# Down projection of a fused attention and FFN block: three groups of 3, 4 and 4 row blocks instead of 2, 3, 3, 3, and other places for its first weight operands

## Chip, cores and metric

One NeuronCore of one Trainium2 chip runs the whole program in one launch. The metric is device time in microseconds (us), median of several runs. Before the change it is 1469.17 us, three runs, 1468.47 to 1473.25.

## What is computed

One block of a diffusion model on 1024 tokens of width 1024, with 256 context tokens: modulation vectors from a condition, neighbourhood attention over a 16 x 64 grid with 16 heads, and a gated FFN of width 2816 with a depthwise convolution. Only the FFN's second product is touched by the change:

```python
def conv_ffn(h, w_up, conv_w, conv_b, w_down):
    a, g = jnp.split(h @ w_up, 2, axis=-1)
    return (a * jax.nn.gelu(dwconv_centred(g, conv_w, conv_b), approximate=False)) @ w_down

x = x + g1 * y
x = x + g2 * conv_ffn(modulate(rms_norm(x, norm2), sh2, sc2), *ffn)
```

All is in float32. Each operand of a large product is split into a rounded high part and a low rest, and a product is three matmuls: high by high, high by low, low by high.

## The kernel before, in words

Both FFN products are done in the seven-product scheme for 2 x 2 blocks (Strassen and Winograd): seven block products with pre-added operands instead of eight. Seven products of one kind are called **ops** here, by the numbers 1 to 7 in the program.

**Up projection** (`up_part`, `up_mm`, line 744). It runs over 11 pairs of hidden row blocks (`i`) and two halves (`part` 1 is g, 0 is a); each op is 12 matmuls into a PSUM bank. Its moving operands `b<op>h`, `b<op>l` stay in SBUF all through: ops 1, 2 and 5 and so on fill 12 places of tag `bA`, then 10 places of `bB`, then 6 of `wa`. A place comes free when the last pair (`i` = 10) has used it. In the last pair PE runs ops 1, 2, 5, 7, 6, then 3, 4. `conv` (line 791) is six taps on DVE for each hidden block, lines 766 and 770 combine the products, and `finish` (804 to 813) writes the seven pre-added forms of the result to `act_dram`.

**Down projection** (`down_mm`, lines 912 to 914). It contracts over 11 row blocks `c`, in groups of `GROUPS` = 2, 3, 3, 3. For each group the ops run in the order `DORD` = 2, 1, 5, 6, 3, 7, 4; an op has four output tiles `j`, and for each the blocks of the group, three matmuls each, into one bank. So an op of a group of n blocks is 12n matmuls, the whole 924. At the end of each bank the sum is moved into `acc` in SBUF: by ACT in the first group for ops 2, 5, 6, 4 (919), else by a DVE add (931). Two sets of four banks take turns; the fourth of both sets lies in one tile, `dx`, which also holds the up projection's `sw`. In the last group DVE and POOL multiply by the gate (927, 928) and POOL issues the output's DMAs (929).

Operands come from two helpers. `prep_a` (872 to 874) loads `da` from `act_dram` (256 KB each, SP queue), ACT rounds it (873), DVE or POOL subtracts to get the low part (874); places `bA`, three ops ahead. `prep_b` (898, 899) takes the raw weights `dr` (loaded at 865, 512 KB each, into places `x1` and `wa`), pre-adds in place on DVE (890, 892, 894, 896), rounds on ACT and subtracts; `db` lies in places `bB`, two ops ahead. DVE makes the low parts for ops 2, 1 and 7, POOL for 5, 6, 3 and 4. While POOL does that, in the last op of the last group but one it also multiplies by the gate and adds the residual (933, 934, eight instructions).

What sets the order on each engine: the program is recorded as written and a scheduler then orders each engine's instructions by its own estimate; each engine runs its queue in order. A place of a tag is given out in turn, and who takes it next waits until its last reader is done.

## Time and profile before

| | |
|---|---|
| runs, median | 1469.17 us (1468.47, 1473.25, 1469.17) |
| the profiled execution | 1474.2 us |
| its span, first to last instruction | 1472.4 us |
| granted TensorE clock, mean | 0.977 |
| DVE busy | 1194.9 us (81%) |
| ACT busy | 746.1 us (51%) |
| POOL busy | 795.0 us (54%) |

The profile is one execution on the chip. Times are from the span's start. A row of the timeline gives start, duration, engine, line, operation, `out<-in`, and in brackets the idle time ahead of it with what ended it. Matmuls overlap, so their start-to-start distance counts, not the printed duration. The down projection is what runs after 1231.83 us.

### The profile page before, as it was taken

What the parts mean: (1) busy time and instruction counts of PE and PEld (TensorE: products, weight loads), DVE (VectorE), ACT (ScalarE), POOL (GpSimd) and SP (SyncE); (2) the same over time, 40 slices, a digit from 0 to 9 for tenths busy, and PEclk for the clock granted to TensorE, in tenths of its full rate; (3) what the DMA queues carried; (4) which work ended last, traced back from release to release, by engine and by line L of the source; (5) the groups of instructions that cost most, each with busy time, mean ns of one, the idle gap of its engine ahead of it and who ended that gap; (6) DMA issues with size and microseconds to landing.
All of it is one profiled execution on the core that took longest, in us unless ns stands there. A gap on an engine that the chain in (4) does not pass through costs nothing. (4 is left out here: it accounts for less than half of the span.)

```text
span 1472.4 us, 22076 instructions
## 1 busy us (share of the span) xinstructions
PE 1371.8 (93%) x7396; PEld 1196.7 (81%) x7396; DVE 1194.9 (81%) x2375; ACT 746.1 (51%) x1617; POOL 795.0 (54%) x687
## 2 busy tenths in 40 slices
PE   6699999999999999998996999999999998999996
PEld 2589889898989899897885777888878876788885
DVE  6788878888888878876579889888888778778877
ACT  6665645555555656654466534444334335545430
POOL 1554644544454546744358645555455545277596
PEclk9899999999999999999998999999999999999998
DMA  9611221313131202253142233333332234644336
GB/s 316 175 37 51 73 81 52 97 48 104 46 104 51 76 14 73 71 129 97 30 128 87 95 100 108 108 108 108 108 108 99 102 116 152 233 145 127 122 98 103
DMA packets 84825, 150.12 MB, mean 102 GB/s; under 512 B 9944, under 2 KB 49000, under 8 KB 84712
## 3 DMA queue, kind: packets, MB, share of 16 engines
q1 hardware_dynamic: 82984, 145.57, 31.1%
q0 software_dynamic: 1728, 3.15, 1.6%
q8 instruction: 58, 0.95, 0.3%
q14 instruction: 55, 0.45, 0.1%
HBM read 115.91 MB, written 32.78 MB: 101 GB/s over the span
## 5 line engine op out<-in xcount | busy, mean ns | idle before, releaser
L692 POOL TENSOR_TENSOR u<-ur,u 128x512 fp32r<-128x512 f32 x154 | 229.4, 1504 | 189.5 <-ACT u L691 181.1
L419 POOL TENSOR_TENSOR p<-p,m 128x640 f32<-128x640 f32 (+1 forms) x128 | 157.3, 1230 | 157.8 <-DVE m L415 121.0
L303 PE MATMUL pq<-wh,hth 128*128 128x384 f32 (+1 forms) x640 | 219.8, 343 | 14.7 <-DVE kn L342 12.9
L307 PE MATMUL pq<-wh,htl 128*128 128x384 f32 (+1 forms) x640 | 215.3, 336 | 2.0 <-DVE htl L196 1.0
L305 PE MATMUL pq<-wl,hth 128*128 128x384 f32 (+1 forms) x640 | 214.9, 336 | 0.5 <-POOL wl L149 0.5
L414 ACT ACTIVATE p<-p,m 128x640 f32<-128x640 f32 (+1 forms) x128 | 102.9, 804 | 83.8 <-DVE m L412 74.4
L691 ACT ACTIVATE u<-ur 128x512 fp32r<-128x512 f32 x154 | 93.1, 627 | 97.4 <-PE sw L744 38.8
L303 PEld LDWEIGHTS pq<-wh,hth 128*128 128x128 f32 x640 | 125.1, 195 | 20.6 <-DVE kn L342 9.3
L327 POOL TENSOR_TENSOR qss<-qss,mhalf 128x4 f32<-128x4 f32 (+1 forms) x80 | 79.9, 999 | 96.9 <-DVE qss L326 82.7
L307 PEld LDWEIGHTS pq<-wh,htl 128*128 128x128 f32 x640 | 124.6, 195 | 2.5 <-DVE htl L196 2.5
L305 PEld LDWEIGHTS pq<-wl,hth 128*128 128x128 f32 x640 | 124.9, 195 | 1.6 <-issue 0.9
L791 DVE SCALAR_TENSOR_TENSOR y<-g,cw,y 128x896 f32<-128x896 f32 (+1 forms) x132 | 104.7, 858 | 21.2 <-ACT y L785 21.2
L899 POOL TENSOR_TENSOR db<-dr,db 128x512 fp32r<-128x512 f32 x44 | 65.6, 1512 | 54.6 <-ACT db L898 44.9
L451 PE MATMUL po<-pt,v 128*128 128x256 f32 x352 | 93.1, 292 | 2.2 <-DVE pt L439 2.2
L450 PE MATMUL po<-pt,v 128*128 128x256 f32 x352 | 93.9, 290 | 0.1
L412 DVE CUSTOM_DVE_ANT_0 p<-s,bias 128x640 f32<-128x640 f32 x96 | 78.4, 816 | 9.4 <-PE s L401 8.8
L898 ACT ACTIVATE db<-dr 128x512 fp32r<-128x512 f32 x77 | 47.3, 629 | 74.7 <-PE dx L914 37.3
L874 POOL TENSOR_TENSOR da<-da 128x512 fp32r<-128x512 f32 x44 | 67.9, 1591 | 29.1 <-ACT da L873 29.0
L438 ACT ACTIVATE pt<-pl 128x384 fp32r<-128x384 f32 (+1 forms) x128 | 58.0, 461 | 46.3 <-PE pl L431 45.3
L473 DVE SCALAR_TENSOR_TENSOR macc<-mr,cs,macc 128x256 f32<-128x256 f32 x112 | 65.4, 584 | 12.3 <-DMA mr<-in_w_mod_dram 11.5
L439 DVE TENSOR_TENSOR pt<-pl,pt 128x384 fp32r<-128x384 f32 (+1 forms) x128 | 65.4, 516 | 6.6 <-ACT pt L438 6.2
L451 PEld LDWEIGHTS po<-pt,v 128*128 128x128 f32 x352 | 66.6, 189 | 3.9 <-DVE pt L439 3.5
(272 smaller groups left out, 4163.8 us busy)
## 6 DMA issues: line engine op xcount, KB each, us to landing
ur<-in_w_up_dram SPq DMA_DIRECT2D x44, 512.0 KB
da<-act_dram SPq DMA_DIRECT2D x77, 256.0 KB
mr<-in_w_mod_dram SPq DMA_DIRECT2D x128, 128.0 KB
dr<-in_w_down_dram SPq DMA_DIRECT2D x22, 512.0 KB
wraw<-in_w_qkv_dram SPq DMA_DIRECT2D x56, 192.0 KB
mraw<-in_w_mod_dram SPq DMA_DIRECT2D x16, 512.0 KB
act_dram<-sa SPq DMA_DIRECT2D x11, 512.0 KB
act_dram<-y SPq DMA_DIRECT2D x11, 512.0 KB
```

The costliest lines, as they stand in the source:

```text
L303: PE.matmul(pq[:, c0:], hth[t][:, k, :], wh[:, c0:], start=(k == 0), stop=False)
L305: PE.matmul(pq[:, c0:], hth[t][:, k, :], wl[:, c0:], start=False, stop=False)
L307: PE.matmul(pq[:, c0:], htl[t][:, k, :], wh[:, c0:], start=False, stop=(k == KC - 1))
L327: POOL.tensor_tensor(ss[:, 4 - n:], ss[:, 4 - n:], mhalf[:, 4 - n:], ALU.pow)
L412: DVE.tensor_tensor_reduce(out=dst, in0=src, in1=bb, scale=1.0, scalar=3e38, op0=ALU.add, op1=ALU.min, accum_out=m[:, 0:1])
L414: ACT.activation(w[:, :n], w[:, :n], AF.Exp, bias=m[:, 0:1], scale=-1.0, accum_out=m[:, 1:2])
L419: POOL.tensor_tensor(w[:, :n], w[:, :n], m[:, 2:3].broadcast_to([P, n]), ALU.mult)
L450: PE.matmul(po, v, th[:, j].rearrange("p a b -> p (a b)"), start=(m == 0), stop=False)
L451: PE.matmul(po, v, tl[:, j].rearrange("p a b -> p (a b)"), start=False, stop=(m == len(blks) - 1))
L691: ACT.activation(s[:, 0], r[op], AF.Copy)
L692: POOL.tensor_tensor(s[:, 1], r[op], f(s[:, 0]), ALU.subtract)
L791: DVE.scalar_tensor_tensor(o, i, w, o, ALU.mult, ALU.add)
```

## The change

The 11 row blocks go in groups of 3, 4 and 4. The `db` operands of the very first op lie in `bA` (the places of the up projection's ops 1 and 2) and no longer in `bB`. Only three blocks of the next group are loaded at op 6; a fourth follows after op 4's operands.

```diff
-GROUPS = [2, 3, 3, 3]
+GROUPS = [3, 4, 4]
...
         if op == RL and n + 1 < len(groups):
-            for c in groups[n + 1]:
+            for c in groups[n + 1][:3]:
                 load_raw(c)
         for c in groups[n]:
-            s = usb.tile([P, 2, HALF], F32R, tag="bB", bufs=10, name=f"db{c}_{op}")
+
+            tag, bufs = ("bA", 12) if q == 0 else ("bB", 10)
+            s = usb.tile([P, 2, HALF], F32R, tag=tag, bufs=bufs, name=f"db{c}_{op}")
...
             opb[op, c] = s
+        if op == DORD[-1] and n + 1 < len(groups):
+            for c in groups[n + 1][3:]:
+                load_raw(c)
```

The lines behind it move by two to five: 890 becomes 892, 899 becomes 901, 912 to 914 become 917 to 919, 931 becomes 936. The matmuls stay 924, the loads 22 and 77; the moves into `acc` go from 112 to 84, all 28 of them DVE adds.

How the order changes, in three places. **DVE where the down projection begins.** `y_1` are the taps of the last pair's convolution, `db_2` and `da_2` the low parts of op 2's operands. Before:

```order
L874 TENSOR_TENSOR da_1_13569<-da_1_13569 128x512
L791 SCALAR_TENSOR_TENSOR y_1_13289<-g_1_13287,cw,y_1_13289 128x128x7
L791 SCALAR_TENSOR_TENSOR y_1_13289<-g_1_13287,cw,y_1_13289 128x112
L791 SCALAR_TENSOR_TENSOR y_1_13289<-g_1_13287,cw,y_1_13289 128x15
L766 TENSOR_TENSOR tmp_0_13427<-pa_2_13426,tmp_0_13427 128x512
L874 TENSOR_TENSOR da_1_13573<-da_1_13573 128x512
L791 SCALAR_TENSOR_TENSOR y_1_13289<-g_1_13287,cw,y_1_13289 128x112
L791 SCALAR_TENSOR_TENSOR y_1_13289<-g_1_13287,cw,y_1_13289 128x15
L791 SCALAR_TENSOR_TENSOR y_1_13289<-g_1_13287,cw,y_1_13289 128x128x7
L770 TENSOR_TENSOR y_0_13288<-tmp_0_13427,y_0_13288 128x512
L899 TENSOR_TENSOR db_2_13549<-dr_1_13543,db_2_13549 128x512
L899 TENSOR_TENSOR db_2_13552<-dr_1_13547,db_2_13552 128x512
```

Now, a little earlier in the queue (`y_0` are the taps of the block before):

```order
L901 TENSOR_TENSOR db_2_13553<-dr_1_13543,db_2_13553 128x512
L901 TENSOR_TENSOR db_2_13556<-dr_1_13547,db_2_13556 128x512
L892 TENSOR_TENSOR dr_0_13680<-dr_0_13680 128x512
L791 SCALAR_TENSOR_TENSOR y_0_13288<-g_0_13286,cw,y_0_13288 128x112
L791 SCALAR_TENSOR_TENSOR y_0_13288<-g_0_13286,cw,y_0_13288 128x15
L901 TENSOR_TENSOR db_2_13559<-dr_1_13551,db_2_13559 128x512
L791 SCALAR_TENSOR_TENSOR y_0_13288<-g_0_13286,cw,y_0_13288 128x128x7
L764 TENSOR_TENSOR g_1_13287<-sw,tmp_1_13293 128x512
L874 TENSOR_TENSOR da_2_13571<-da_2_13571 128x512
L874 TENSOR_TENSOR da_2_13575<-da_2_13575 128x512
```

The three `db_2` stand ahead of all six taps of `y_1` and of line 770; `db_1` now is what follows line 770 and the last `da_1`.

**SP's queue, the first group's `da`.** Before, the loads for six ops stand together, ahead of the last `y_0` store:

```order
L872 DMA da_1_13573<-act_dram 128x512
L872 DMA da_5_13577<-act_dram 128x512
L872 DMA da_5_13581<-act_dram 128x512
L872 DMA da_6_13602<-act_dram 128x512
L872 DMA da_6_13606<-act_dram 128x512
L872 DMA da_3_13658<-act_dram 128x512
L872 DMA da_3_13662<-act_dram 128x512
L872 DMA da_7_13700<-act_dram 128x512
L872 DMA da_7_13704<-act_dram 128x512
L804 DMA act_dram<-y_0_13288 128x512
```

Now only ops 2, 1 and 5 stand there, since nine `da` and three `db` fill the 12 places:

```order
L872 DMA da_5_13603<-act_dram 128x512
L804 DMA act_dram<-y_0_13288 128x512
...
L865 DMA dr_0_14173<-in_w_down_dram 128x1024
L812 DMA act_dram<-sa_13526 128x1024
L805 DMA act_dram<-y_1_13289 128x1024
L872 DMA da_6_13628<-act_dram 128x512
L872 DMA da_6_13632<-act_dram 128x512
L872 DMA da_6_13636<-act_dram 128x512
```

Op 6's `da` moved behind seven weight loads (six left out) and two stores of the up projection's last pair.

**POOL in the last group, where op 3 ends.** Before:

```order
L929 DMA out_dram<-acc_13585 16x8x512
L928 TENSOR_TENSOR acc_13586<-acc_13586,g2b 128x512
L899 TENSOR_TENSOR db_3_14983<-dr_1_14447,db_3_14983 128x512
L929 DMA out_dram<-acc_13587 16x8x512
L899 TENSOR_TENSOR db_3_14986<-dr_1_14451,db_3_14986 128x512
L928 TENSOR_TENSOR acc_13588<-acc_13588,g2b 128x512
L874 TENSOR_TENSOR da_4_15053<-da_4_15053 128x512
L929 DMA out_dram<-acc_13586 16x8x512
```

Now:

```order
L901 TENSOR_TENSOR db_3_14876<-dr_1_14179,db_3_14876 128x512
L874 TENSOR_TENSOR da_3_14801<-da_3_14801 128x512
L874 TENSOR_TENSOR da_3_14805<-da_3_14805 128x512
L874 TENSOR_TENSOR da_3_14809<-da_3_14809 128x512
L934 DMA out_dram<-acc_13608 16x8x512
L901 TENSOR_TENSOR db_3_14879<-dr_1_14183,db_3_14879 128x512
L901 TENSOR_TENSOR db_3_14882<-dr_1_14451,db_3_14882 128x512
L934 DMA out_dram<-acc_13610 16x8x512
L901 TENSOR_TENSOR db_4_15037<-dr_1_14175,db_4_15037 128x512
```

Two of the gate multiplications and two output DMAs of op 1 stand further ahead, among op 6's operands, and four splits of each kind stand where three stood.

## The prediction

> **What bounds the kernel now.** I read the busy shares first, then the down projection in stretches (columns: PE, PEld, DVE, ACT, POOL busy with counts, granted clock, DMA share, GB/s), then PE's own waits after 1170 us.

> ```profile
> PE 1371.8 (93%) x7396; PEld 1196.7 (81%) x7396; DVE 1194.9 (81%) x2375; ACT 746.1 (51%) x1617; POOL 795.0 (54%) x687
> ```
> ```profile
> 1231.80:1238.10 6.30, 0.41 (x2) 0.00 (x0) 6.30 (x5) 5.14 (x10) 6.20 (x5) 0.84 0.11 42
> 1238.10:1242.60 4.50, 4.44 (x9) 2.82 (x10) 4.50 (x5) 0.45 (x1) 2.79 (x2) 0.50 0.00 0
> ...
> 1260.00:1434.00 174.00, 174.00 (x769) 144.10 (x768) 134.04 (x167) 83.47 (x136) 116.29 (x81) 1.00 0.42 134
> ...
> 1445.50:1451.40 5.90, 5.89 (x14) 4.64 (x15) 5.83 (x5) 0.19 (x1) 5.48 (x5) 0.52 0.20 20
> ```
> ```profile
> PE dpo L913 <- DVE db L899: 5.9, 1, 5.9
> PE dx L912 <- DVE acc L931: 5.5, 1, 5.5
> PE dx L912 <- DVE tmp L766: 1.7, 1, 1.7
> ...
> PE dpq L913 <- POOL db L899: 0.5, 1, 0.5
> ```

> PE is the bound: from 1260 to 1434 it never stops, 769 matmuls in 174 us, **0.2263 us** each. Neither weights nor DMA limit that stretch. What can be won lies in the two ends, so I add up PE's lost time there from its timeline.

> ```profile
> 1231.83 0.39 PE L912 MATMUL dpo<-db,da 128*128 128x512 f32 x1
> 1238.12 0.79 PE L913 MATMUL dpo<-db,da 128*128 128x512 f32 x1 [5.91 <-DVE db L899]
> ...
> 1245.98 0.39 PE L744 MATMUL pa<-b3h,u 128*128 128x512 f32 x1
> ...
> 1253.91 0.39 PE L914 MATMUL dpq<-db,da 128*128 128x512 f32 x1
> 1256.00 0.50 PE L912 MATMUL dx<-db,da 128*128 128x512 f32 x1 [1.70 <-DVE tmp L766]
> ...
> 1439.63 0.39 PE L914 MATMUL dpo<-db,da 128*128 128x512 f32 x1
> 1445.51 0.79 PE L912 MATMUL dx<-db,da 128*128 128x512 f32 x1 [5.49 <-DVE acc L931]
> ...
> 1451.43 0.39 PE L914 MATMUL dtr<-db,da 128*128 128x512 f32 x1
> ...
> 1466.39 0.39 PE L914 MATMUL dx<-db,da 128*128 128x512 f32 x1
> ```

> From 1231.83 to 1466.39 are 234.6 us. 924 down matmuls and 24 of up ops 3 and 4 are 947 steps of 0.2263, 214.3 us; **20.3 us are lost**. At the beginning: the wait, 6.29 - 0.23 = 6.06; then 24 matmuls (5.43) take 7.86 at the halved clock of the second stretch, 2.43 lost; together 8.5. At `dx`: 2.09 - 0.23 = 1.86. At the end: 0.6 on POOL's split, 5.88 - 0.23 = 5.65 at `dx`, then 14 steps (3.17) take 5.92, 2.75 lost; together 9.0. The last 0.9 is spread.

> **The change, part by part.**

> *First weight operands.* The wait at 1231.83 is for `db_2`'s low part, and DVE's own queue made it late:

> ```profile
> 1220.40 0.69 DVE L890 TENSOR_TENSOR dr<-dr 128x512 f32<-128x512 f32 x1 [0.97 <-DMA dr<-in_w_down_dram]
> 1221.01 1.66 DVE L791 SCALAR_TENSOR_TENSOR y<-g,cw,y 128x112 f32<-128x112 f32 x3
> ...
> 1225.42 0.69 DVE L874 TENSOR_TENSOR da<-da 128x512 fp32r<-128x512 f32 x1 [0.95 <-ACT da L873]
> 1226.55 1.68 DVE L791 SCALAR_TENSOR_TENSOR y<-g,cw,y 128x896 f32<-128x896 f32 x3 [0.44 <-ACT y L785]
> ...
> 1229.90 4.82 DVE L791 SCALAR_TENSOR_TENSOR y<-g,cw,y 128x112 f32<-128x112 f32 x3
> 1234.64 1.75 DVE L770 TENSOR_TENSOR y<-tmp,y 128x512 f32<-128x512 f32 x1
> 1236.32 3.44 DVE L899 TENSOR_TENSOR db<-dr,db 128x512 fp32r<-128x512 f32 x2
> ```
> ```profile
> 1228.12 9.40 POOL L874 TENSOR_TENSOR da<-da 128x512 fp32r<-128x512 f32 x6 [10.14 <-ACT da L873]
> ```

> Three taps take 1.66 us with POOL quiet and 4.82 beside POOL's splits (1.57 each); the adds of two SBUF tiles go from 0.69 to 1.75. After the change the three `db_2` (0.6 apart, 1.8) go into DVE's gaps of 0.97, 0.95 and 0.44, so `y_1`'s taps start at about 1226.6 as now. Behind them stand taps 1.68, line 766 0.6, three taps 1.66, `da_2` and three `da_1` 2.4, line 770 0.6: 6.94, to 1233.5. POOL cannot slow them before about 1233, for its first work, op 5's `da`, is now rounded on ACT behind two `db_1`, the second in the place that up op 6 holds to 1232. `db_1`'s first low part comes at 1234.2 alone, and up to 2.8 later if that split, line 770 and the last `da_1` meet POOL (1.1 more for most of them). PE needs it after nine `dpo` and three `dtr` matmuls, 1231.83 + 12 x 0.2263 = 1234.5. So the new wait is 0 to 2.5 us; I take 1.5, and no halved clock, since the 1.70 us wait at 1256.00 was followed by none. **Saved: 8.5 - 1.5 = 7.0.**

> *`dx` behind the up projection.* Now DVE has op 7's first pre-add ahead of the read of `sw` (line 766), and that pre-add waits for POOL's tenth split: 1233.2 + 10 x 1.57 = 1248.9, then 1.7 and 0.7: 1251.3. PE comes after 79 matmuls, 1231.83 + 17.9 + 1.5 = 1251.2. Between 0 and 4 us (POOL at 1.9 a split, as in a row below); I take 1.0. **Saved: 0.9.**

> *Op 6's `da` behind SP's stores.* Its DMA can go at about 1255, after the `y_1` store that waits for DVE's last line 770.

> ```profile
> 1269.02 1.01 SPq L872 DMA_DIRECT2D da<-act_dram  x2
> ```
> ```profile
> 1272.36 1.28 ACT L873 ACTIVATE da<-da 128x512 fp32r<-128x512 f32 x2 [0.60 <-DMA da<-act_dram]
> ```

> The second of these was issued by 1270.0 and used at 1272.36: at least 2.4, at most 3.4 us. With two stores and three loads in the way I put it at 1259.5 and POOL's split at 1261.4. PE has 45 matmuls after `dx` (op 2's rest, op 5, op 1's last bank), 10.2 us from 1251.8: 1262. Cost 0 with 0.6 us to spare; upper bound 4.

> *Group size.* 28 DVE adds go, 0.68 each (19 us of DVE):

> ```profile
> L931 DVE TENSOR_TENSOR acc<-dtr,acc x33: 674/678/692, 1258.3 to 1443.4; 128x512 f32<-128x512 f32 x33
> ```

> They lie beside a PE that never stops, so by themselves they are worth nothing. Four blocks leave less room: 12 places are three ops of `da`, 10 are two and a half of `db`. In the middle groups a `db` place comes back about 13 us before its next use (one op of 48 matmuls, 10.9, plus the last bank), and POOL makes eight splits for ops 5, 6 and 3 in that time, 8 x 1.44 (116.29 / 81) = 11.5: hidden, at most 2 us per group at 1.75 a split. The fourth block's weights are asked for after op 4's operands, an op or more ahead.

> *The end.* What held PE at 1445.51:

> ```profile
> 1423.12 1.76 DVE L894 TENSOR_TENSOR dr<-dr 128x512 f32<-128x512 f32 x1 [1.19 <-POOL db L899]
> ...
> 1433.02 8.46 DVE L894 TENSOR_TENSOR dr<-dr 128x512 f32<-128x512 f32 x1 [2.93 <-POOL db L899]
> ...
> 1444.77 0.68 DVE L931 TENSOR_TENSOR acc<-dx,acc 128x512 f32<-128x512 f32 x1
> ```
> ```profile
> 1399.40:1434.48 35.08, 35.08 (x156) 28.89 (x154) 26.67 (x27) 12.62 (x21) 35.08 (x26) 1.00 0.36 99
> ```
> ```profile
> 1433.22 1.88 POOL L899 TENSOR_TENSOR db<-dr,db 128x512 fp32r<-128x512 f32 x1
> ...
> 1440.00 1.70 POOL L929 DMA_DIRECT2D out_dram<-acc  x1
> ```

> One pre-add stood 8.46 us, exactly while POOL had no gap, and the move out of `dx` stood behind it. POOL was behind because the last group's 24 splits share it with the residual, gate and output work. That extra work stays the same, but the group's PE time grows from 84 x 3 to 84 x 4 matmuls (57 to 76 us). POOL's string is 35.08 / 26 = 1.35 us each; from the residual of the third bank (2 us ahead of the group) to op 3's last `db` are 33 instructions, 44.6 us, 42.6 into the group; PE wants it at 4 x 10.9 + 2.0 = 45.5. So op 3 does not wait, and op 7 has 10.9 us behind it. Between two uses of `dx` lie three banks, 27 matmuls (6.1 us) before and 36 (8.15) now. The same 8.46 us pre-add would hold PE 5.49 - 2.04 = 3.45 us. Bounds 0 and 9; I take 3.4. **Saved: 5.6.**

> [...]

> **Sum:** 7.0 + 0.9 + 5.6 = 13.5 off the profiled execution's 1474.2 us: 1460.7. That execution stands 5.0 above the median. If its excess is one of the waits removed here, runs after come out at 1460.7; if it lies ahead of 1231, at 1455.7. I say **1460**, nearer the first, as the waits are what I can see.

> **Rivals.**
> - *The wait moves to the next operands of the first group:* `db_1` (2.5 instead of 1.5), `dx` (4 instead of 1) and op 6's `da` (2 instead of 0): 6 more, 1466. For it: POOL at 1.9 a split. Against: POOL starts later than now.
> - *The end stays as it is:* 9.0 instead of 3.4, 1466.
> - *Slower: DVE starves behind POOL at both ends.* Mechanism: the 8.46 us row. At the beginning POOL has six splits in a row (1233.2 to 1242.6); a `db_1` held for all of it gives 8.1 us and 2.75 of clock, 9.3 more than taken. At the end the string is four instructions longer, 9.0 + 5.4 instead of 3.4, 11 more. 1481. It decides once a pre-add stands longer than `dx`'s 8.15 us. Against: in 174 us without a stop DVE got in after one POOL instruction nearly always.
> - *The early splits are not early,* because their weights land late: 8.5 stays, 1468.

> **Chances.** Forecast (1454 to 1464.5) 0.58, first rival 0.16, second 0.14, slower 0.08, last 0.04. The range 1454 to 1469 leaves out the slower case and the tails. About 0.3% (4.4 us) is what a measurement can tell from no change. Faster by more, below 1464.8: the forecast and a good third of the rivals at 1466, 0.70; within 0.19; slower 0.11.

> **What would show it.** Right: PE's first `dpo` has no wait, its first wait is for `db_1`, under 3.4 us, with clock 1.00; POOL's first split starts near 1233; PE runs through groups 2 and 3; a `dx` wait near the end under 4 us. Wrong: a wait of PE on `da` or POOL inside the 4-block groups, a stretch at 0.50 near 1238, or a DVE pre-add over 8 us with PE idle behind it.

## The result, and the profile after

The changed kernel takes 1463.95 us (median of 13 runs, 1458.21 to 1468.27); the kernel before, beside it, 1472.22 us (13 runs, 1467.62 to 1474.77). The ratio is 0.9948, 95% interval 0.9935 to 0.9961: 7.7 us faster by the ratio. The profiled execution took 1463.59 us, its span is 1461.8. Of the experiments' executions one, of e2, took 7620 us; the ratios leave it out. Busy shares hardly moved; DVE's busy time fell from 1194.9 to 1184.4 us, by less than the 19 us of the 28 adds:

```profile
PE 1368.4 (94%) x7396; PEld 1193.9 (82%) x7396; DVE 1184.4 (81%) x2347; ACT 741.8 (51%) x1617; POOL 797.4 (55%) x687
```

PE's waits in the down projection, all of them (line, what it waited for, us in total, times, longest):

```profile
PE dx L917 <- DVE acc L936: 2.7, 1, 2.7
PE dpq L917 <- DVE tmp L766: 2.0, 1, 2.0
PE dx L917 <- DVE tmp L766: 1.3, 1, 1.3
PE sw L744 <- DVE tmp L778: 0.2, 1, 0.2
```

The wait of 5.9 us at the first `dpo` is gone, and none for `db_1` has come. The one near the end is 2.7 instead of 5.5 us. New is a wait for a bank, `dpq`. PE's timeline at these places, and four stretches (columns as in the prediction; the third from the end is the granted clock):

```profile
1230.17 0.39 PE L917 MATMUL dpo<-db,da 128*128 128x512 f32 x1
...
1248.80 0.53 PE L917 MATMUL dpq<-db,da 128*128 128x512 f32 x1 [2.03 <-DVE tmp L766]
...
1253.97 0.50 PE L917 MATMUL dx<-db,da 128*128 128x512 f32 x1 [1.26 <-DVE tmp L766]
...
1418.90 0.50 PE L917 MATMUL dx<-db,da 128*128 128x512 f32 x1 [2.73 <-DVE acc L936]
...
1455.80 0.39 PE L919 MATMUL dx<-db,da 128*128 128x512 f32 x1
```
```profile
1230.17:1248.00 17.83, 16.36 (x70) 12.61 (x68) 14.12 (x16) 6.63 (x12) 15.87 (x9) 1.00 0.38 128
1248.80:1252.50 3.70, 3.70 (x9) 2.59 (x9) 3.70 (x4) 0.35 (x1) 2.16 (x2) 0.54 0.57 231
1254.00:1415.00 161.00, 161.00 (x710) 133.28 (x711) 123.33 (x130) 75.89 (x129) 113.28 (x79) 1.00 0.47 151
1418.90:1423.34 4.44, 4.44 (x12) 3.49 (x13) 4.44 (x6) 2.18 (x4) 2.28 (x3) 0.62 0.79 139
```

From 1230.17 to 1455.80 are 225.6 us. The same 214.3 us of matmuls as in the prediction leave **11.3 us lost**, against 20.3 before: 9.0 less. The other 1.66 us of the two executions' difference lie ahead: the first down matmul started at 1230.17, not at 1231.83. The lost time after: at the beginning the `dpq` wait (2.19), nine matmuls at the half clock behind it (1.50), `dx` (1.63), 0.38 at up op 4 and 1.0 spread, 6.7 in all; at the end `dx` (2.89) and twelve matmuls that took 4.44 us instead of 2.72, 4.6 in all. In the middle PE never stops for 161 us. What stands behind the wait near the end, DVE's pre-add and its move out of `dx`, and two output DMA issues of POOL ahead of them:

```profile
1409.68 7.97 DVE L896 TENSOR_TENSOR dr<-dr 128x512 f32<-128x512 f32 x1 [4.57 <-POOL db L901]
...
1418.17 0.68 DVE L936 TENSOR_TENSOR acc<-dx,acc 128x512 f32<-128x512 f32 x1
```
```profile
1402.70 1.01 POOL L934 DMA_DIRECT2D out_dram<-acc  x1
...
1405.95 1.14 POOL L934 DMA_DIRECT2D out_dram<-acc  x1
```

### The profile page after: what moved, and what is told of

It reads as the page before. It is cut to its first block, busy times and chain, and to the rows that moved or that the text cites. A ratio compares the mean times of both kernels' runs of the same rounds, so it can differ in the third digit from the quotient of the medians.

```text
span 1461.8 us, 22048 instructions
## 1 busy us (share of the span) xinstructions
PE 1368.4 (94%) x7396; PEld 1193.9 (82%) x7396; DVE 1184.4 (81%) x2347; ACT 741.8 (51%) x1617; POOL 797.4 (55%) x687
## 5 line engine op out<-in xcount | busy, mean ns | idle before, releaser
L791 DVE SCALAR_TENSOR_TENSOR y<-g,cw,y 128x896 f32<-128x896 f32 (+1 forms) x132 | 101.7, 835 | 21.2 <-ACT y L785 21.2
L874 POOL TENSOR_TENSOR da<-da 128x512 fp32r<-128x512 f32 x44 | 71.0, 1658 | 36.3 <-ACT da L873 36.3
```

Of the source, the lines that this page charges most:

```text
L791: DVE.scalar_tensor_tensor(o, i, w, o, ALU.mult, ALU.add)
```

## The experiments

Twelve kernels were run. How they stand, with three numbers of each profiled execution: its first down matmul, PE's lost time as above, and the tail from the start of the last matmul to the end of the span.

| kernel | ratio to before (95%) | first | lost | tail |
|---|---|---|---|---|
| before | 1 | 1231.83 | 20.3 | 6.0 |
| whole change | 0.9948 (0.9935 to 0.9961) | 1230.17 | 11.3 | 6.0 |
| e1, groups alone | 0.9996 (0.9983 to 1.0010) | 1234.74 | 19.2 | 6.1 |
| e2, places alone | 0.9998 (0.9985 to 1.0010) | 1230.66 | 18.7 | 6.0 |
| e5, e2 without POOL's early work | 0.9938 (0.9922 to 0.9954) | 1229.97 | 11.7 | 6.0 |
| e3, `dx` as two tiles | 0.9962 (0.9949 to 0.9975) | 1230.08 | 10.1 | 8.7 |
| e7, op 3's `db` on DVE | 0.9966 (0.9951 to 0.9982) | 1232.54 | 16.9 | 6.0 |
| e6, e3 and e7 together | 0.9926 (0.9908 to 0.9944) | 1234.21 | 7.2 | 7.2 |
| e9, without op 1's output DMAs | 0.9938 (0.9918 to 0.9957) | 1231.27 | 10.6 | 6.1 |
| e4, without six pre-adds | 0.9940 (0.9928 to 0.9953) | 1234.12 | 7.5 | 6.1 |
| e8, e6 and three pre-adds on POOL | 0.9930 (0.9910 to 0.9950) | 1232.77 | 9.2 | 7.2 |

The first down matmul comes anywhere from 1229.97 to 1234.74, though these kernels are nearly alike up to there. One execution's span therefore says little about 4 us; lost time and tail of one trace, and the ratio over several runs, say more. The sum of lost time and tail, taken from that of before, foretells the ratio within 2 us (0.0014) for every kernel but e4.

**The two parts of the change.** e1 leaves the first `db` in its old place, e2 leaves the groups:

```diff
e1: -            tag, bufs = ("bA", 12) if q == 0 else ("bB", 10)
    +            tag, bufs = "bB", 10
e2: -GROUPS = [3, 4, 4]
    +GROUPS = [2, 3, 3, 3]
```

> Only the groups of 3, 4 and 4; the first db operands lie in bB as in the kernel before. In the two traces PE's lost time from the first dpo to the last matmul is 20.3 us before and 11.3 after (beginning 10.9 and 6.7, end 9.0 and 4.6). Theory (two separate gains: places at the beginning, longer groups at the end): PE stands at its first dpo again, 5 to 8 us behind DVE's db low part, with the clock at half afterwards, and the end loses about 4.6 as with the whole change; time 3 to 5 us under the kernel before, ratio about 0.997. Rival (the groups bring it all, by fewer moves into acc and less work on DVE): ratio 0.995 as with the whole change.

> Only the places of the first db operands; groups of 2, 3, 3 and 3 as before. Theory: no wait at the first dpo and no stretch at half clock right behind it; the end as before, a dx wait of about 5.5 us with 2.75 of half clock; 3 to 6 us under the kernel before, ratio about 0.997, and the savings of this and of the groups alone add up to the 8.3 us of the whole change within 2. Rival (the wait moves to db_1 or dx when a group is only two blocks, 6 dpo and 24 dtr matmuls): no gain, ratio 1.000.

Neither is shown to be faster than before. In e1 the wait at `dpo` is longer than before (8.4 us, not 5.9), since three `db_2` now stand behind the taps, and so is the one at `dx` (6.2, not 5.5). In e2 the wait is gone at `dpo` and back at `db_1`: the rival. PE's two longest waits in e1, then in e2:

```profile
PE dpo L918 <- DVE db L901: 8.4, 1, 8.4
PE dx L917 <- DVE acc L936: 6.2, 1, 6.2
```
```profile
PE dtr L918 <- DVE db L901: 5.6, 1, 5.6
PE dx L917 <- DVE acc L936: 5.5, 1, 5.5
```

So the gain is not a sum of two. What the two parts do together shows on DVE and POOL where POOL's first split meets DVE's row. In e2 (DVE, then POOL):

```profile
1227.47 0.67 DVE L766 TENSOR_TENSOR tmp<-pa,tmp 128x512 f32<-128x512 f32 x1
1228.08 1.73 DVE L874 TENSOR_TENSOR da<-da 128x512 fp32r<-128x512 f32 x1
1229.73 2.69 DVE L791 SCALAR_TENSOR_TENSOR y<-g,cw,y 128x112 f32<-128x112 f32 x2
...
1236.68 3.42 DVE L901 TENSOR_TENSOR db<-dr,db 128x512 fp32r<-128x512 f32 x2
```
```profile
1227.96 8.25 POOL L874 TENSOR_TENSOR da<-da 128x512 fp32r<-128x512 f32 x5 [11.15 <-ACT da L873]
```

And after the whole change (the first line is an edge of the convolution):

```profile
1228.55 0.27 DVE L791 SCALAR_TENSOR_TENSOR y<-g,cw,y 128x15 f32<-128x15 f32 x1
1228.71 0.71 DVE L874 TENSOR_TENSOR da<-da 128x512 fp32r<-128x512 f32 x1
...
1230.98 0.70 DVE L770 TENSOR_TENSOR y<-tmp,y 128x512 f32<-128x512 f32 x1
1231.58 0.71 DVE L874 TENSOR_TENSOR da<-da 128x512 fp32r<-128x512 f32 x1
1232.18 1.91 DVE L901 TENSOR_TENSOR db<-dr,db 128x512 fp32r<-128x512 f32 x3
```
```profile
1229.61 5.63 POOL L874 TENSOR_TENSOR da<-da 128x512 fp32r<-128x512 f32 x1 [13.29 <-ACT da L873]
```

In e2 the two took turns: DVE's subtractions in these rows lasted 1.73 and 1.7 us, POOL's 1.65. After the change DVE ran on at 0.70 and POOL's *first* subtraction stood for 5.63 us, until DVE paused at 1234.09. The three `db_1` took 1.91 us and PE waited for none. Whether POOL's work is what holds `db_1` in e2 was tried by leaving it out, in e2's kernel:

```diff
+            if n or op in DA:
                 (DVE if op in DA else POOL).tensor_tensor(s[:, 1], f(s[:, 1]), f(s[:, 0]), ALU.subtract)
```

> The places alone (groups of 2, 3, 3 and 3) as in the second experiment, and in the first group the low parts of da for ops 5, 6, 3 and 4 are left out (POOL's eight subtractions; those parts of the sums are not computed rightly). With the places alone PE waited 5.6 us for db_1, whose DVE queue ran beside POOL's first subtractions from 1227.96 on. Theory (POOL's start ahead of DVE's row is what made db_1 late; where the first group has three blocks POOL starts inside DVE's row and is the one that waits): without those subtractions DVE's queue runs at 0.6 us each, the db_1 wait is under 1.5 us, no half clock there; 6 to 9 us under the kernel before, ratio 0.994 to 0.996. Rival (DVE's queue is too long for two blocks in any case, or ACT is late): a db_1 wait of 4 us or more, ratio 1.000.

As the theory had it: no wait for `db_1` at all; the ratio is 0.9938 (0.994 to 0.996 expected). With two blocks DVE's queue was short enough where POOL stayed away: the two `db_1` took 1.31 us together, 3.42 in e2. (A `dpq` wait of 1.7 us on line 766 came in its place, not foreseen.)

**The end.** The fourth banks become two tiles (e3, with PSUM pools split so that the sizes fit); op 3's four splits of the last group go from POOL to DVE (e7); both (e6):

```diff
-    X = [tr[0], tr[1], tr[2], xt[:, 0]]
-    Y = [pq[0], pq[1], po, xt[:, 1]]
+    X = [tr[0], tr[1], tr[2], xt[0]]
+    Y = [pq[0], pq[1], po, xt[1]]
...
-            (DVE if op in DB else POOL).tensor_tensor(s[:, 1], src, f(s[:, 0]), ALU.subtract)
+            (DVE if op in DB or (n == len(groups) - 1 and op == 3) else POOL).tensor_tensor(s[:, 1], src, f(s[:, 0]), ALU.subtract)
```

> The whole change, but the fourth banks of the two sets, which lie in one tile dx of two banks, become two tiles. Theory (the dx wait near the end is for op 5's fourth bank, moved out behind DVE's 8-us pre-add, while PE wants op 6's fourth bank, moved out 15 us earlier; the shared tile makes the wait): DVE's pre-add beside POOL still takes 5 to 9 us, but PE has no wait for dx there and no half clock, 4 to 5 us under the whole change: ratio to the kernel before 0.991 to 0.992. Rival (DVE being 8 us late is what costs; the wait moves to the next bank or to op 7's operands): the same time as the whole change, ratio 0.995, with a wait of 2 us or more in the same 30 us.

> The same move of op 3's four low parts to DVE in the last group, but dx in one tile as in the whole change. Theory (op 7's first pre-add stood 8 us because it was released alone, by POOL's db split, in the middle of a string of POOL without a pause; now it stands in DVE's own queue): no DVE pre-add over 4 us near the end, no dx wait, no half clock there; 4 us under the whole change, ratio to the kernel before 0.991 to 0.993. Rival (a DVE instruction is stuck there whichever it is): a DVE row over 6 us and a dx wait of 2 us or more stay, ratio 0.995.

> The whole change, dx as two tiles, and in the last group the four low parts of op 3's db on DVE instead of POOL. Theory (with dx split POOL's string is what the end waits for: 2.6 us of PE at op 4's db, and an output DMA issued 2.3 us later, landing 8.6 us behind; four subtractions of 1.25 us off POOL bring it 5 us earlier, and op 7's pre-adds no longer wait for POOL): no PE wait over 1 us after 1400, last matmul about 7 us plus 214.3 after the first, end 6 us behind it; 4 to 6 us under the whole change, ratio to the kernel before 0.990 to 0.992. Rival (DVE takes the place of POOL: four more subtractions beside POOL's at 1.7 us make its moves out of PSUM or its db_7 late): a PE wait on DVE of 2 us or more near the end, ratio 0.995.

In e3 DVE's pre-add stood even longer, and PE did not wait for it. After 1400 it waited for POOL alone, and POOL's last output DMA left later (tail 8.7 us). DVE's timeline of e3, then PE's waits after 1400:

```profile
1410.11 11.35 DVE L900 TENSOR_TENSOR dr<-dr 128x512 f32<-128x512 f32 x1 [4.60 <-POOL db L905]
```
```profile
PE dtr L922 <- POOL db L905: 2.6, 2, 2.0
```

So the shared tile was the way by which the stuck DVE instruction reached PE (theory): a wait of 2.73 us in the whole change, none here beside a row of 11.35. But in this trace the time it saved was given back to POOL's string (rival): 0.9962, no gain on the whole change. e7 went the rival's way. The first of the moved splits, which waited for nothing of POOL's, stood 11.33 us in DVE's own queue, and PE waited 5.1 us for `dx`. That row of e7:

```profile
1409.63 11.33 DVE L901 TENSOR_TENSOR db<-dr,db 128x512 fp32r<-128x512 f32 x1
```

e6 has the same stuck row (11.33 us) and no PE wait over 0.3 us after 1400. Its ratio 0.9926 is the best of all; its interval overlaps that of the whole change, so it is not shown to beat it.

**What holds DVE beside POOL, and the clock.** Three kernels of their own. The first asks both questions (its code shortened here):

```python
p = [op(POOL, z, hi) for _ in range(10)]   # 128x512 subtractions, SBUF to SBUF
d = op(DVE, p[1], hi)                      # released by POOL's second; other cases vary this
```

> A kernel of its own; it computes nothing of the block. Part one, subtractions of SBUF tiles of 128x512: ten on POOL without a pause, and beside them one on DVE that is released by POOL's second, or by one, two or four small ACT copies behind it; six of DVE in a row; one of DVE with a PSUM source; one with a PSUM source and one from SBUF behind it; twelve of DVE in a row with four of POOL released by DVE's third, without and with a PSUM source in DVE's seventh; and ten of POOL with a DMA issue in the middle, one of DVE beside them. Theory (the engine that runs without a pause keeps the shared access to SBUF; a DMA issue or a PSUM source lets the other in): the single DVE subtraction stands 8 to 10 us in the first cases and 5 us with the DMA issue, 0.7 us from PSUM; POOL's first subtraction stands until DVE's row ends (7 us), or until the seventh (3 us). Rival (they take turns after each instruction): every DVE subtraction 1.7 us beside POOL, and POOL's 1.7 beside DVE, in all cases. Part two, 15 rows of 48 matmuls with pauses of 0.5 to 6 us between them, each length twice. Theory (the clock is halved after pauses of 2 us and more, for 3.4 us: 2.03 and 2.73 us did, 1.70 and 1.26 did not): no half clock behind pauses under 1.7 us, half clock behind all over 2.1. Rival (what decides is where in a fixed period the pause falls): the two pauses of a length differ.

The rival held for DVE beside POOL: a subtraction of DVE took 1.74 us beside POOL, one of POOL up to 1.71 beside DVE, one of DVE from PSUM 0.69, and none of DVE's rows beside POOL stood longer than 1.80 us. The DMA issue meant for the middle of the last string ran only at 140.58, as the ten subtractions ended (140.64), so this kernel does not show what an issue does. A string of ten on POOL without a pause did not hold DVE by itself here. For the clock, the pauses between rows of 48 matmuls and the granted clock (third column from the end) in the 5 us behind them. PE's timeline has the pauses of 1.47, 2.04 and 2.62 us in brackets; each came a second time in the same order:

```profile
179.61 0.50 PE L121 MATMUL tb<-mz,wr 128*128 128x512 f32 x1 [1.47 <-ACT mz L128]
192.84 0.50 PE L121 MATMUL tb<-mz,wr 128*128 128x512 f32 x1 [2.04 <-ACT mz L128]
208.21 0.50 PE L121 MATMUL tb<-mz,wr 128*128 128x512 f32 x1 [2.62 <-ACT mz L128]
```
```profile
179.61:184.61 5.00, 5.00 (x22) 4.14 (x23) 0.00 (x0) 0.41 (x1) 0.00 (x0) 1.00 0.00 0
192.84:197.84 5.00, 5.00 (x15) 3.97 (x16) 0.00 (x0) 0.41 (x1) 0.00 (x0) 0.66 0.01 3
208.21:213.21 5.00, 5.00 (x22) 4.17 (x23) 0.00 (x0) 0.41 (x1) 0.00 (x0) 1.00 0.00 0
...
277.84:282.84 5.00, 5.00 (x22) 4.14 (x23) 0.00 (x0) 0.41 (x1) 0.00 (x0) 1.00 0.00 0
291.07:296.07 5.00, 5.00 (x15) 3.99 (x16) 0.00 (x0) 0.41 (x1) 0.00 (x0) 0.66 0.00 0
306.52:311.52 5.00, 5.00 (x12) 3.93 (x13) 0.00 (x0) 0.41 (x1) 0.00 (x0) 0.50 0.02 3
```

Pauses of 0.3, 0.9 and 1.47 us did not cost the clock (six of six, 1.00), 2.04 did both times (0.66), 2.62 once not and once for longer, 3.48 and 4.34 all four times. In the whole kernels a pause of 2.03 to 2.07 us cost it in four traces (whole change, e3, e6, e7) and not in e9, where the clock behind 2.07 us was 1.00. So of these pauses some of 2.03 us and more cost the clock and some did not, and length alone does not decide it. That the place of the pause does, as the rival has it, fits the two of 2.62 us, which differed, but was not shown.

The whole kernel's POOL has output DMA issues in its string; the first test had none there. That was the second test's question:

```diff
+            if i in dmas:
+                POOL.dma_start(out=out[o:o + 16, 0:HALF], in_=z[:16, :])
```

> A kernel of its own; it computes nothing of the block. The first one showed DVE and POOL taking turns (1.74 and 1.70 us) in every case, where the whole kernel shows 8 and 11 us. In the whole kernel POOL's rows behind an output DMA issue last 1.57, behind two 1.87, at starts 1.25 us apart, so one begins before the other ends; without such an issue they last 1.28. Cases: ten subtractions on POOL and one on DVE (one case: four) released by POOL's sixth, with no DMA issue, one behind POOL's third, one each behind the third and fifth, two together behind the third, one behind the third and one behind the eighth; then rows of eleven on DVE with two of POOL released by DVE's third, plain, with a long scalar_tensor_tensor (128x896) as the fourth, with rounded outputs from the fifth on, and with both. Theory (a DMA issue on POOL lets its next instructions overlap, and DVE gets no turn until POOL pauses or issues again): no issue 1.75 us; one issue or two ahead 4 to 6 us, to the end of the ten; with one behind the eighth about 3 us; POOL's rows 1.55 us and 1.85 us. Rival (turns are kept whatever is issued): 1.75 us in all cases. For the rows of DVE: POOL's first stands over 4 us where the long instruction or the rounded outputs are in the row, 1.6 in the plain one; rival: 1.6 in all.

DVE's rows of this kernel: no issue, one behind POOL's third, one each behind the third and the fifth, then one behind the third and one behind the eighth, and no issue again (the cases left out gave 5.39 too):

```profile
20.69 1.73 DVE L55 TENSOR_TENSOR dca<-ca,xs 128x512 f32<-128x512 f32 x1 [7.72 <-POOL ca L55]
34.36 5.39 DVE L55 TENSOR_TENSOR dcb<-cb,xs 128x512 f32<-128x512 f32 x1 [11.94 <-POOL cb L55]
48.66 5.38 DVE L55 TENSOR_TENSOR dcc<-cc,xs 128x512 f32<-128x512 f32 x1 [8.91 <-POOL cc L55]
...
92.19 5.95 DVE L55 TENSOR_TENSOR dcf<-cf,xs 128x512 f32<-128x512 f32 x1 [8.36 <-POOL cf L55]
105.96 1.73 DVE L55 TENSOR_TENSOR dcg<-cg,xs 128x512 f32<-128x512 f32 x1 [7.83 <-POOL cg L55]
```

One DMA issue in POOL's string, three subtractions ahead of DVE's request, and DVE stood until POOL's ten were done: 5.39 us beside the four that were left, 1.73 without the issue. A later issue did not let it in (5.95, where 3 was expected). POOL's rows behind the issue lasted 1.26 us as always, so the overlap of rows, which the theory read in the whole kernel, is not the sign of it. The long multiply-add and the rounded outputs in rows of DVE brought nothing like it (POOL's first took 1.55 to 2.04 us). The third test asked for the short ones:

> A kernel of its own; it computes nothing of the block. In the whole change POOL's first split at the beginning took 5.63 us beside DVE's rows, which ran at full speed; in the kernel before, and with the groups or the places alone, DVE was the one slowed. The long multiply-add and the rounded outputs did not bring this about in the last kernel. Left: the short multiply-adds of the convolution's edges (128x15), which stand in DVE's queue some rows ahead. Rows of DVE of 128x512, POOL's two subtractions released by the third: plain; with one or two 128x15 multiply-adds behind the first; with 128x112 and 128x15 there; with 128x15 there and a PSUM source three rows behind the release; with 128x15 behind the release. Then ten subtractions on POOL, with none, one or three of 128x15 behind the third, and one of DVE released by the sixth. Theory (a short instruction lets the next ones overlap, as a DMA issue does on POOL, and the engine that overlaps gives no turn): POOL's first stands 4 to 6 us, until DVE's row ends, where a short one is ahead of its release, about 3 us with the PSUM source, 1.6 where it is behind or absent; DVE's one stands 4 to 6 us behind a short one on POOL. Rival (turns are kept): 1.6 to 1.75 us in all.

POOL's first subtraction beside a plain row of DVE, with one 128x15 multiply-add ahead of the release, with two, with one ahead and a PSUM source behind, and with one behind the release:

```profile
14.08 1.57 POOL L55 TENSOR_TENSOR pra<-ra,z 128x512 f32<-128x512 f32 x1 [13.64 <-DVE ra L55]
22.73 5.19 POOL L55 TENSOR_TENSOR prb<-rb,z 128x512 f32<-128x512 f32 x1 [5.42 <-DVE rb L55]
31.86 5.19 POOL L55 TENSOR_TENSOR prc<-rc,z 128x512 f32<-128x512 f32 x1 [2.71 <-DVE rc L55]
...
50.06 1.58 POOL L55 TENSOR_TENSOR pre<-re,z 128x512 f32<-128x512 f32 x1 [2.57 <-DVE re L55]
57.98 1.72 POOL L55 TENSOR_TENSOR prf<-rf,z 128x512 f32<-128x512 f32 x1 [4.68 <-DVE trf L78]
```

With a short DVE instruction ahead in the row POOL stood until the row was done (5.19 us); with one behind the release turns were kept (1.72). With a PSUM source in the row POOL got its turn at once (1.58), not first at that instruction as the theory said. Short instructions on POOL held nobody (DVE 1.74). The beginning of the changed kernel looks like this (POOL stood 5.63 us there): its row had a 128x15 edge of the convolution 1.06 us ahead of POOL's start and no PSUM source behind it; in e2 POOL started ahead of that edge, during a PSUM read. In the whole kernel itself the edge was not taken out, so there this cause is argued from the test and not shown.

In the whole kernel the DMA issues were taken out of the stretch before the stuck pre-add:

```diff
-                POOL.dma_start(out=ov[t, :, :, c], in_=d, accum_op=ALU.add)
+                if op != 1:
+                    POOL.dma_start(out=ov[t, :, :, c], in_=d, accum_op=ALU.add)
```

> The whole change, with op 1's four output DMAs of POOL in the last group left out (that quarter of half the output stays without its FFN part); POOL's string of subtractions there is otherwise the same. Theory (these DMA issues, at 1402.70 and 1405.95 in the trace after, are what kept DVE's pre-add waiting 8 us): no DVE row over 3 us from 1400 to 1420, PE's dx wait under 0.5 us and no half clock there, 4 to 5 us under the whole change, ratio to the kernel before 0.991 to 0.993. Rival (POOL's string without a pause is enough): the pre-add stands 6 us or more, the dx wait 2 us or more, ratio 0.995.

```profile
1411.86 1.77 DVE L896 TENSOR_TENSOR dr<-dr 128x512 f32<-128x512 f32 x1 [3.13 <-POOL db L901]
1413.55 0.68 DVE L937 TENSOR_TENSOR acc<-dpo,acc 128x512 f32<-128x512 f32 x1
1416.07 1.76 DVE L896 TENSOR_TENSOR dr<-dr 128x512 f32<-128x512 f32 x1 [1.84 <-POOL db L901]
```

(DVE's timeline of e9.) The same pre-add takes 1.77 us and PE's half clock at the end is gone; the end loses 1.3 instead of 4.6 us (a `dx` wait of 1.2 stays, as the second pre-add waits for POOL's splits). But the execution lost 2.6 more at the beginning, where its code is that of the whole change, and the ratio shows no gain over it. That the pre-add stood 7.97 us with the issues and 1.77 without them is shown; that this is worth 4 us of time is not.

**The wait left at the beginning.** e4 leaves out the first group's pre-adds of ops 6 and 4, which stand on DVE ahead of line 766; e8 moves op 4's three to POOL in e6's kernel:

```diff
e4: +            if op == 6 and n:
    +            if op == 4 and n:
e8: -                DVE.tensor_tensor(b21, b21, b12, ALU.subtract)
    +                (DVE if n else POOL).tensor_tensor(b21, b21, b12, ALU.subtract)
```

> The whole change, with the six pre-adds of ops 6 and 4 left out in the first group (that part of the sums is not computed). They stand on DVE ahead of the read of the last up products (line 766). Theory (in the trace after, PE waits 2.03 us for dpq, 1.6 more at half clock and 1.26 for dx, because that read stands behind pre-adds of 1.7 us each beside POOL): the dpq wait goes, no half clock there, 3.5 to 5 us under the whole change, ratio to the kernel before about 0.992. Rival (DVE is held by POOL in any case, or line 770 behind line 766 sets it): a dpq or dx wait of 1.5 us or more stays and the time is within 1.5 us of the whole change.

> The whole change, dx as two tiles, the last group's low parts of op 3's db on DVE, and in the first group op 4's three pre-adds on POOL instead of DVE. Theory (PE's wait for dpq, 2.1 us, 1.4 more at half clock, and 1.3 to 1.6 for dx come from DVE's read of the last up products behind six pre-adds; three of them go, 4 us of DVE's queue): the dpq wait under 0.7 us, no half clock there, dx wait under 1 us; 3 to 5 us under the kernel with dx and op 3's move, ratio to the kernel before 0.989 to 0.991. Rival (POOL is later by three pre-adds, 4 to 5 us, and PE waits for op 6's or op 5's low parts): a wait on POOL of 2 us or more near 1260, ratio 0.993 or above.

In e4's trace both waits of the beginning and the half clock there are gone: lost time 7.5 against 11.3 us, the end unchanged (`dx` wait 2.7). So the pre-adds are what made PE wait there (2.03 us for `dpq` and 1.26 for `dx` with them). The time does not show it (0.9940), and this is the one kernel where lost time and ratio differ by 3.9 us; with five runs that stays open. In e8 the `dpq` wait fell to 0.8, but three subtractions more on POOL slowed what DVE has next to 1.75 us each, and `dx` waited 4.4. PE's two longest waits in e8:

```profile
PE dx L921 <- DVE tmp L768: 4.4, 1, 4.4
PE dpq L921 <- DVE tmp L768: 0.8, 1, 0.8
```

No gain over e6: the work was moved, and the meeting of the two engines with it.

## Why the prediction was right, and where it was not

The forecast was 13.5 us off the profiled execution, 1460.7, told as 1460. The lost time fell by 9.0, and 1.66 more lay ahead of the down projection: 1463.59. The range held. The 1.66 us are no term of the prediction, and they are smaller than the scatter of the first down matmul in the table: to that extent the figure is luck. Errors of both signs met in the rest: the first step saved 1.5 more than said, the second cost 4.3 more, the end saved 1.2 less. By its own steps:

- *First weight operands, 7.0 saved.* No wait at the first `dpo`, as said, and no half clock there; the wait for `db_1` put at 1.5 was 0. The size is about right, the reason only in part. POOL was to stay away until about 1233, but started at 1229.61, inside DVE's row. Where the two took turns, in e2, `db_1` cost 5.6 us and the clock (0.50 behind it). What saved it is that POOL was the one that stood, which no step of the prediction had. (The prediction counts 24 matmuls behind the old wait; the trace has 23, so 0.2 us more were lost to the clock there.) The rival "the wait moves to the next operands" is what the places do alone.
- *`dx` behind the up projection, 1.0.* **Under-sized, the largest miss.** It was 5.3: a `dpq` wait of 2.19, 1.50 of half clock and 1.63 at `dx`. The step followed only line 766's read of `sw`. The read of `pa` stands in the same queue ahead of it, and its bank is the second `dpq`, which PE wants earlier still, since nothing held it at `db_1`. That read stood behind pre-adds beside POOL, and without them both waits are gone (e4).
- *Op 6's `da`, 0.* Right: SP issued it at 1256.48 (about 1255 said), POOL split it from 1262.62, and PE had no wait.
- *Group size, nothing by itself.* Right: e1's ratio is 0.9996, and the 4-block groups ran 161 us without a stop.
- *The end, 3.4.* It lost 4.6. The mechanism was right: a pre-add of 7.97 us (8.46 before), the move out of `dx` behind it, a wait of 2.89 (3.45 said). Mis-sized was the clock: 1.72 at half speed behind a wait of 2.73 us (granted clock 0.62), for which the step added nothing. Nor does the longer group fix the end: with the same groups the pre-add stood 11.25 us in e1, and the end lost 7.9 (6.39 of wait, 1.52 of clock). The 9.0 to 4.6 of the profiled execution has luck in it. By the prediction's own signs it was close: a pre-add over 8 us with PE idle behind it would have shown it wrong.
- *DVE beside POOL, and the clock.* The end step read one pre-add that stood 8.46 us exactly while POOL had no gap. Beside a string of ten on POOL without a gap DVE stood 1.74 us (m1), POOL beside DVE up to 1.71; with a DMA issue ahead on POOL DVE stood 5.39 to 11.35 us (m2 and the whole kernels), and with a short instruction ahead on DVE POOL stood 5.19 (m3). No run shows the prediction's limit of 3.4 us for a wait with the clock at 1.00: the clock was halved behind 2.03 us in the whole change and behind 2.04 twice of two in m1, and behind 2.62 once of two.
- *The median.* The profiled execution before stood 5.0 us above the three runs' median; over 13 runs the median is 1472.22, 2.0 below that execution. The lower of the two readings, 1455.7, came from a median of three that was low.

## What to carry to other kernels

Two edits that were not shown to be worth anything alone (0.9996 and 0.9998) were worth 7.7 us together, by way of which of two engines waited for the other: test the parts apart before crediting either. Read every bank and every operand that stands in the late engine's queue, not only the one that showed the last wait; the next one is wanted earlier once the first is gone. Where DVE has something urgent beside a string of POOL's SBUF work, look for DMA issues in that string (DVE stood 5.39 us with one in m2, 1.73 without), and look for accumulators that are drained at different times but share a tile: taking out the one (e9) shortened PE's `dx` wait near the end here from 2.73 to 1.18 us and taking out the other (e3) ended it, though neither is shown to have saved time over the whole change.
